# Expert weights loaded through two DMA queues instead of one, and the bias row selection copied by ScalarE instead of GpSimd

## The chip, the cores and the metric

The kernel runs on one core of a Trainium2 chip. The metric is the time of one execution on the device in microseconds (us): the median of a few runs. One execution was also profiled; its page and its trace are what this document reads. Engines are named as in the profile: PE is TensorE, PEld its weight loads, DVE is VectorE, ACT is ScalarE, POOL is GpSimd, SP is SyncE, which here does nothing but issue DMAs.

## The reference, cut to what matters

One encoder layer on 256 tokens of width 1024, in float32. A mixer part (three branches, gates, a projection, a layer norm) gives `h`. Then 32 experts of which each token takes 4:

```python
logits = hf @ w_router + b_router
top_val, top_idx = lax.top_k(logits, 4); top_w = softmax(top_val)
# for each expert e, on the tokens that chose it:
gu = xb @ w_gu[e] + b_gu[e]                       # (n, 1024) @ (1024, 2048)
gate, up = split(gu); gate = min(gate, 7); up = clip(up, -7, 7)
act = (up + 1) * (gate * sigmoid(1.702 * gate))
out = (act @ w_down[e] + b_down[e]) * weight      # (n, 1024) @ (1024, 1024)
# summed into the tokens, then h = LN(2**0.25 * h + sum)
```

The weights of all 32 experts (w_gu 8 MB and w_down 4 MB each) are read once, 384 MB in all.

## The kernel before, in words

The mixer comes first and lasts until about 320 us. The experts then go in 16 pairs, p = 0 to 15. Each expert has 64 places for tokens, so a pair fills the 128 rows of the PE's output: expert e of the pair has rows 64e to 64e+63, and `pair_mm` (line 1001) issues one matmul for each half.

For a pair, `up` (line 1007) makes the gate and up products in four PSUM tiles `gps` (128x512 each) over eight steps k. Before step 0 (for p = 0 after the last step) `add_bias` (line 992) adds the bias: a small tile `sel` picks row 2p and 2p+1 out of the bias rows by a matmul (lines 995 and 998). After the last step `swiglu` (line 808) runs twice: DVE takes the minimum (L809), ACT the sigmoid (L810), DVE the rest (L811 to L813). `down` (line 1056) begins with `add_bias` on two tiles `yps`, then runs eight steps on `w_down`; in its middle the tokens of the next pair are gathered (`gather`, L847 and L938). `transpose_act` (L1044, L1045), `weigh` (L946 to L955) and `combine` (L1078, L1082) follow.

The order is a pipeline: `up(p)`, then `down(p-1)` with `gather(p+1)` inside, then `transpose_act(p)`, `weigh(p)`, `combine(p-1)`, then `up(p+1)`. The whole loop stands inside `tc.manual_schedule` for DVE, PE and ACT: these three engines execute their instructions in the order in which the program writes them. Instructions of POOL and SP are placed by the scheduler, unless `keep_in_program_order` pins them.

The weights come in pieces of 2048 KB, twelve for a pair: eight of `w_gu` (`load_gu`, line 789) and four of `w_down` (`load_down`, line 800). They go round ten buffers ("ring0" to "ring9", `new_unit`, line 777), so a piece can be issued when the piece ten places before it has been used up. All are issued by SP, one after the other. From the third pair on, piece i of a pair holds two steps' rows of one expert: i even is the first expert of the pair, i odd the second, so that PE needs pieces 2j and 2j+1 together for steps 2j and 2j+1. For p < 2 and for the last two w_gu pieces of the last pair, one piece serves one step for both experts (`both`, line 784); the w_down pieces of pair 14 serve two steps for both experts each (`rows`). The last pair's w_down comes in twelve smaller pieces in `last_down` (line 1103), by SP. At p = 8, `norm_rows` (line 1129) selects the rows of the closing layer norm's parameters in the same way as `add_bias`.

Of the kernel before, what the change touches and what calls it, by code (L numbers as in the profile page):

```python
# [13 lines left out]
AF = mybir.ActivationFunctionType  # L14
# [762 lines left out]
def new_unit(K, shape):  # L777

    i = K.slot_no % K.NRING
    K.slot_no += 1  # L780
    return (K.early if i in K.EARLY else K.ring[i]).tile([128, *shape], F32, name="wexp", tag=f"ring{i}")


def both(p, k):

    return p < 2 or (p, k // 2) == (NE // 2 - 1, 3)


def load_gu(K, A, p, i, w=None):

    if (p, i) in K.loaded:
        return K.loaded[p, i]
    w = K.loaded[p, i] = w or new_unit(K, (2, 2 * D))
    src = A["w_gu"][0, 2 * p:2 * p + 2, i // 2 * 256:i // 2 * 256 + 256].rearrange("e (p k) n -> p e k n", p=128)
    src = src[:, :, i % 2] if both(p, i) else src[:, i % 2]
    K.tc.keep_in_program_order(K.nc.sync.dma_start(w, src))
    return w


def load_down(K, A, p, i, rows=False):  # L800

    w = new_unit(K, (2, 2, D) if rows else (4, D))
    src = A["w_down"][0, 2 * p:2 * p + 2, i // 2 * 512:i // 2 * 512 + 512].rearrange("e (p k) n -> p e k n", p=128)
    K.nc.sync.dma_start(w, src[:, :, i % 2 * 2:i % 2 * 2 + 2] if rows else src[:, i % 2])
    return w


# [9 lines left out]
def moe(ctx, K, A):  # L817
    tc, nc = K.tc, K.nc
# [122 lines left out]
    def weigh(p, P):  # L941

        bank = yps if p == 0 else mps if p == NE // 2 - 1 else gps
        t = bank()
        for tau in range(2):
            nc.tensor.transpose(t[:, tau * 128:tau * 128 + 128], P[:, tau].rearrange("p e s -> p (e s)"), K.ident)  # L946
        G = big.tile([128, S], F32R, name="G", tag="G", bufs=2)
        nc.scalar.activation(G, t[:, :S], AF.Copy)
        t = bank()
        for tau in range(2):  # L950
            nc.tensor.matmul(t[:, 0:2], P[:, tau].rearrange("p e s -> p (e s)"), wts[:, tau, 2 * p:2 * p + 2],
                             start=tau == 0, stop=tau == 1)
        w = big.tile([128, 1], F32, name="sw", tag="sw", bufs=2)
        for e in range(2):
            nc.scalar.activation(w[e * 64:e * 64 + 64], t[e * 64:e * 64 + 64, e:e + 1], AF.Copy)  # L955
        return G, w


    for p, k in [(p, k) for p in range(2) for k in range(8)][:K.NRING + 2]:
        if (p, k) not in ((0, 7), (1, 2)):  # L960
            load_gu(K, A, p, k)
    K.loaded[0, 7] = [big.tile([128, 2 * D], F32, name="wexp", tag=tag, bufs=1) for tag in ("work", "y")]
    for k, w in enumerate(K.loaded[0, 7]):
        nc.sync.dma_start(w, A["w_gu"][0, k, 768:1024].rearrange("(p k) n -> p k n", p=128)[:, 1])
    load_gu(K, A, 1, 2, K.res.tile([128, 2, 2 * D], F32, name="wexp", tag="sum", bufs=1))

    xT, P = gather(0, P0), P0
# [24 lines left out]
    def add_bias(acc, p, at, first):  # L992

        t = big.tile([128, 2, 64], F32, name="sel", tag="sel", bufs=2)
        nc.gpsimd.tensor_copy(t, K.rows[:, 2 * p:2 * p + 2, None].broadcast_to([128, 2, 64]))  # L995
        for ac, (r0, c0) in zip(acc, at):
            r = slice(r0, r0 + 32)
            nc.tensor.matmul(ac, t[r].rearrange("k e s -> k (e s)"), bias[r, c0:c0 + ac.shape[-1]], start=first,  # L998
                             stop=not first, skip_group_check=True)
# [7 lines left out]
    def up(p, xT, between=None, inside=None):  # L1007

        g = [(yps if p == 0 and n % 2 else gps)() for n in range(4)]
        early = p > 0  # L1010
        if early:
            add_bias(g, p, GU_ROWS, True)
        for k in range(8):
            if k % 2 == 0:
                ws = [load_gu(K, A, p, k + e) for e in range(2)]
            for n in (0, 2, 1, 3):
                cols = slice(n * 512, n * 512 + 512)
                if both(p, k):
                    w = ws[k % 2]
                    rows = [w[e][:, cols] if isinstance(w, list) else w[:, e, cols] for e in range(2)]  # L1020
                else:
                    rows = [w[:, k % 2, cols] for w in ws]
                pair_mm(g[n], xT, k, rows, not early and k == 0, early and k == 7)
            if inside and k == 6:
                inside()
        if not early:
            add_bias(g, p, GU_ROWS, False)
        if p == 0:
            K.work = big.tile([128, 2, D], F32, name="work", tag="work", bufs=1)
        if between:  # L1030
            between()
        a = K.work[:, 0]
        t = big.tile([128, 4, 512], F32, name="sg", tag="y", bufs=1)
        for i in range(2):
            swiglu(nc, t[:, i], t[:, 2 + i], a[:, i * 512:i * 512 + 512], g[i], g[2 + i])
        return a
# [19 lines left out]
    def down(p, aT, w, between=None):  # L1056
        yy = [yps() for _ in range(2)]
        add_bias(yy, p, DN_ROWS, True)
        for i in range(2):
            rows = p == NE // 2 - 2  # L1060
            ws = [load_down(K, A, p, i * 2 + e, rows) for e in range(2)]
            for k in range(4):
                for n in range(2):
                    c = slice(n * 512, n * 512 + 512)
                    w2 = [ws[k // 2][:, e, k % 2, c] if rows else ws[e][:, k, c] for e in range(2)]
                    pair_mm(yy[n], aT, i * 4 + k, w2, False, i * 4 + k == 7)
            if between and i == 0:
                between()
        y = new_y()
        for n in range(2):  # L1070
            leave(y, yy[n], w, slice(n * 512, n * 512 + 512))
        return y
# [56 lines left out]
    def norm_rows(gb):  # L1129

        t = big.tile([128, 2, 128], F32, name="nsel", tag="P", bufs=2)
        nc.gpsimd.tensor_copy(t, K.rows[:, 0:2, None].broadcast_to([128, 2, 128]))
        for r0, o in zip((64, 96), gb):
            for n in range(2):
                ps = mps()
                nc.tensor.matmul(ps, t[r0:r0 + 2, n], bias[r0:r0 + 2, 512:1024], start=True, stop=True)  # L1136
                nc.scalar.activation(o[:, n * 512:n * 512 + 512], ps, AF.Copy)
# [12 lines left out]
    with tc.manual_schedule(engines={mybir.EngineType.DVE, mybir.EngineType.PE, mybir.EngineType.Activation}):  # L1150
        P1 = choice(1)
        ahead = []
        a = up(0, xT, inside=lambda: ahead.append(gather(1, P1)))
        xT = ahead[0]
        for p in range(1, NE // 2):
            first = []
            a0, a = a, up(p, xT, (lambda: first.append(after(0, a, P))) if p == 1 else None)
            if p == 1:
                held = first[0]
                t = K.res.tile([128, 4, D], F32, name="sum", tag="sum", bufs=1)  # L1160
                z[:], gb = (t[:, 0], t[:, 1]), (t[:, 2], t[:, 3])
            P = P1
            if p < last:
                P1 = choice(p + 1)
                ahead = []
                y = down(p - 1, held[0], held[2], lambda: ahead.append(gather(p + 1, P1)))
                xT = ahead[0]
                now = after(p, a, P)
                if p == NE // 4:
                    norm_rows(gb)  # L1170
                back(y, p - 1, held[1])
                held = now
        G, w = weigh(last, P)
        now = []
        y = down(last - 1, held[0], held[2], lambda: now.extend((transpose_act(last, a, True), last_parts(last))))
        parts = now[1]
        st = last_down(last, now[0], G, w, parts, lambda: back(y, last - 1, held[1]))
        finish(K, A, [K.work[:, 0], K.work[:, 1]], st, *gb)
# [187 lines left out]
```

## Time and profile before

| what | us |
|---|---|
| median of 3 runs (1233.05 to 1233.71) | 1233.61 |
| the profiled execution's own time | 1233.55 |
| its span, first to last instruction | 1231.5 |
| PE busy | 1164.2 |
| DVE busy | 381.3 |
| ACT busy | 260.0 |
| POOL busy | 47.8 |
| q1 (SP's DMA queue), 456.62 MB, share of 16 DMA engines over the span | 90.5% |

The span is what the instructions cover; the execution's own time has about 2 us around it. Busy PE is not PE at its peak. A queue's share is the time that its packets took as a share of what 16 DMA engines have. "q1 hardware_dynamic" is the queue that SP fills, "q10" ACT's, "q0 software_dynamic" the one that POOL fills. A stage is read with the view by stretches: busy time of each engine, the clock granted to PE, the share of the DMA engines that was busy and the rate in GB/s.

### The profile page before, as it was taken

The numbers are of one execution on the slowest core, as the hardware profiler recorded it, in microseconds if no ns is written. First come the engines' busy times: TensorE is split into PE (matmuls) and PEld (weight loads), VectorE is DVE, ScalarE is ACT, GpSimd is POOL, SyncE is SP. The second block draws the span as 40 slices with busy tenths as digits, with TensorE's granted clock in tenths as the row PEclk, the third lists the DMA queues.
The fourth block names the chain that finished last, engine by engine and source line by source line (L and its number), as shares of the span: only waits on it lengthen the run. The fifth ranks groups of instructions, "written<-read, shape, count | busy, mean of one in ns | idle before, by whom it ended". The sixth has DMA issues, their size and how long they took to land.

```text
span 1231.5 us, 14887 instructions
## 1 busy us (share of the span) xinstructions
PE 1164.2 (95%) x6413; PEld 639.3 (52%) x6413; DVE 381.3 (31%) x591; ACT 260.0 (21%) x453; POOL 47.8 (4%) x70
## 2 busy tenths in 40 slices
PE   6999999999999999999989898999898989899995
PEld 6898999998544343443334242434243424333333
DVE  7995465486211131111202030211111111111124
ACT  4775555453111010100101010201010101000010
POOL 2150000000000000000000000000000000000000
PEclk8999999999999999999999999999999999999998
DMA  8755557687999999999999999999999999999994
GB/s 284 254 195 171 193 191 245 254 310 273 384 412 411 395 430 432 428 431 430 430 432 429 431 431 431 431 429 431 431 428 434 429 429 433 429 430 431 427 422 161
DMA packets 77241, 458.24 MB, mean 372 GB/s; under 512 B 4678, under 2 KB 39184, under 8 KB 50292
## 3 DMA queue, kind: packets, MB, share of 16 engines
q1 hardware_dynamic: 76712, 456.62, 90.5%
q8 instruction: 52, 0.85, 0.3%
q10 hardware_dynamic: 332, 0.56, 0.1%
q14 instruction: 17, 0.14, 0.0%
q0 software_dynamic: 128, 0.07, 0.0%
HBM read 456.18 MB, written 1.05 MB: 371 GB/s over the span
## 4 chain that ended last, share of the span: by engine, by line
PE 62%; DMA 34%; DVE 2%; ACT 1%; issue 0%; SPq 0%; POOL 0%; DVEq 0%; ACTq 0%
DMA wexp<-in_w_down_dram 27%; PE gps L1004 16%; PE yps L1004 15%; PE pj L146 7%; PE pj L145 7%; PE pj L144 7%; DMA wexp<-in_w_gu_dram 6%; PE mps L847 5%; PE gps L1044 1%; PE gps L998 1%; DVE wlo L118 1%; PE yps L1078 1%; PE mps L1078 1%; PE yps L998 1%; DMA first<-in_ln_in_b_dram 0%; PE mps L1136 0%
## 5 line engine op out<-in xcount | busy, mean ns | idle before, releaser
L1004 PE MATMUL gps<-wexp,xT 128*64 128x512 f32 x1984 | 447.9, 599 | 36.2 <-DMA wexp<-in_w_gu_dram 36.1
L1004 PEld LDWEIGHTS gps<-wexp,xT 128*64 128x64 f32 x1984 | 144.9, 138 | 335.1 <-issue 281.1
L1004 PE MATMUL yps<-wexp,work 128*64 128x512 f32 x960 | 220.7, 596 | 4.6 <-DMA wexp<-in_w_down_dram 4.6
L809 DVE TENSOR_SCALAR sg<-gps 128x512 f32<-128x512 f32 x31 | 21.3, 688 | 459.9 <-PE gps L1004 426.6
L1004 PEld LDWEIGHTS yps<-wexp,work 128*64 128x64 f32 x960 | 69.3, 137 | 142.9 <-issue 126.5
L118 DVE TENSOR_TENSOR wlo<-wraw,whi 128x1024 fp32r<-128x1024 f32 (+2 forms) x98 | 119.4, 1227 | 61.6 <-ACT whi L117 61.0
L810 ACT ACTIVATE sg<-sg 128x512 f32<-128x512 f32 x32 | 20.2, 630 | 489.1 <-DVE sg L809 489.1
L117 ACT ACTIVATE whi<-wraw 128x1024 fp32r<-128x1024 f32 (+2 forms) x98 | 95.4, 977 | 98.0 <-PE pj L145 82.1
L144 PE MATMUL pj<-hT,whi 128*128 128x256 f32 (+1 forms) x392 | 112.5, 287 | 0.0
L145 PE MATMUL pj<-hT,whi 128*128 128x256 f32 (+1 forms) x392 | 110.6, 282 | 0.3 <-DVE hT L118 0.3
L146 PE MATMUL pj<-hT,wlo 128*128 128x256 f32 (+1 forms) x392 | 110.6, 282 | 0.0
L1051 DVE SCALAR_TENSOR_TENSOR y<-yps,sw,y 128x512 fp32r<-128x512 f32 x30 | 22.5, 751 | 244.9 <-ACT y L1050 243.6
L145 PEld LDWEIGHTS pj<-hT,whi 128*128 128x128 f32 (+1 forms) x392 | 73.7, 188 | 1.0 <-DVE hT L118 0.8
L144 PEld LDWEIGHTS pj<-hT,whi 128*128 128x128 f32 (+1 forms) x392 | 73.7, 188 | 0.9 <-ACT whi L117 0.7
L146 PEld LDWEIGHTS pj<-hT,wlo 128*128 128x128 f32 (+1 forms) x392 | 73.6, 188 | 0.2
L847 PEld LDWEIGHTS mps<-P,h 128*128 128x128 f32 x512 | 61.6, 196 | 12.7 <-issue 12.2
L847 PE MATMUL mps<-P,h 128*128 128x128 f32 x512 | 64.8, 285 | 0.4 <-DVE P L840 0.4
L938 ACT ACTIVATE xT<-mps 128x512 f32<-128x512 f32 x32 | 19.1, 598 | 176.5 <-PE mps L847 176.5
L995 POOL COPY sel<-kp 128x128 f32<-128x128 f32 x32 | 9.5, 298 | 808.2 <-PE yps L998 483.3
L1050 ACT ACTIVATE y<-yps,sw 128x512 fp32r<-128x512 f32 x30 | 20.6, 688 | 88.1 <-PE yps L1004 78.7
L1082 DVE TENSOR_TENSOR sum<-sum,yps 128x512 f32<-128x512 f32 (+1 forms) x30 | 18.8, 666 | 22.1 <-PE yps L1078 22.1
L812 DVE TENSOR_TENSOR sg<-sg 128x512 f32<-128x512 f32 x32 | 22.1, 690 | 3.2 <-ACT sg L810 1.6
(279 smaller groups left out, 1049.3 us busy)
## 6 DMA issues: line engine op xcount, KB each, us to landing
wexp<-in_w_gu_dram SPq DMA_DIRECT2D x127, 2048.0 KB, 37.4
wexp<-in_w_down_dram SPq DMA_DIRECT2D x60, 2048.0 KB, 32.1
wraw<-in_w_in_dram SPq DMA_DIRECT2D x28, 1024.0 KB, 5.5
wexp<-in_w_down_dram SPq DMA_DIRECT2D x8, 768.0 KB, 16.4
wraw<-in_w_mem_kv_dram SPq DMA_DIRECT2D x4, 1024.0 KB
wraw<-in_w_br_gla_dram SPq DMA_DIRECT2D x4, 1024.0 KB
wraw<-in_w_out_dram SPq DMA_DIRECT2D x4, 1024.0 KB, 7.5
wraw<-in_w_br_fnet_dram SPq DMA_DIRECT2D x2, 1024.0 KB
```

Of the source, the lines that this page charges most:

```text
L117: K.nc.scalar.activation(hi, src, AF.Copy)
L118: K.nc.vector.tensor_tensor(lo, src, hi.bitcast(F32), ALU.subtract)
L144: nc.tensor.matmul(out, wh, xh, start=first, stop=False)
L145: nc.tensor.matmul(out, wh, xl, start=False, stop=False)
L146: nc.tensor.matmul(out, wl, xh, start=False, stop=last)
L809: nc.vector.tensor_scalar(g, gate, 7.0, None, ALU.min)
L812: nc.vector.tensor_tensor(g, g, s, ALU.mult)
L847: nc.tensor.matmul(t[:, c], h1[tau][:, f0 + c % 2:f0 + 256:2], P[:, tau].rearrange("p e s -> p (e s)"), start=first and c == 0, stop=last, ...
L998: nc.tensor.matmul(ac, t[r].rearrange("k e s -> k (e s)"), bias[r, c0:c0 + ac.shape[-1]], start=first, stop=not first, skip_group_check=True)
L1004: nc.tensor.matmul(acc[e * 64:e * 64 + 64], xT[:, k, e * 64:e * 64 + 64], w[e], start=first, stop=last, skip_group_check=True)
L1051: nc.vector.scalar_tensor_tensor(y[:, 1, sl], acc, w, y[:, 0, sl].bitcast(F32), ALU.mult, ALU.subtract)
L1078: nc.tensor.matmul(c, G[:, tau * 128:tau * 128 + 128], y[:, i, sl], start=i == 0, stop=i == 1)
```

## The change

In `load_gu`, odd pieces of pairs 2 to 15 are issued by POOL (`nc.gpsimd`) instead of SP. In `load_down`, odd pieces of pairs 1 to 14 are issued by POOL, and all pieces are pinned to program order. In `add_bias` and `norm_rows`, the copy that makes the selection tile is an ACT activation (Copy) instead of a POOL copy.

```diff
@@ load_gu
-    K.tc.keep_in_program_order(K.nc.sync.dma_start(w, src))
+    eng = K.nc.gpsimd if p > 1 and i % 2 else K.nc.sync
+    K.tc.keep_in_program_order(eng.dma_start(w, src))
@@ load_down
-    K.nc.sync.dma_start(w, src[:, :, i % 2 * 2:i % 2 * 2 + 2] if rows else src[:, i % 2])
+    eng = K.nc.gpsimd if p > 0 and i % 2 else K.nc.sync
+    K.tc.keep_in_program_order(eng.dma_start(w, src[:, :, i % 2 * 2:i % 2 * 2 + 2] if rows else src[:, i % 2]))
@@ add_bias
-        nc.gpsimd.tensor_copy(t, K.rows[:, 2 * p:2 * p + 2, None].broadcast_to([128, 2, 64]))
+        nc.scalar.activation(t, K.rows[:, 2 * p:2 * p + 2, None].broadcast_to([128, 2, 64]), AF.Copy)
@@ norm_rows
-        nc.gpsimd.tensor_copy(t, K.rows[:, 0:2, None].broadcast_to([128, 2, 128]))
+        nc.scalar.activation(t, K.rows[:, 0:2, None].broadcast_to([128, 2, 128]), AF.Copy)
```

## Rows read from the trace of the kernel before

**Rows 1.** The page: DMA queue (packets, MB, share) and the chain's shares by engine.
```profile
q1 hardware_dynamic: 76712, 456.62, 90.5%
...
PE 62%; DMA 34%; DVE 2%; ACT 1%; issue 0%; SPq 0%; POOL 0%; DVEq 0%; ACTq 0%
```

**Rows 2.** View by stretches: stretch, length, busy us of engines (instructions), PEclk, DMA share, GB/s.
```profile
320.00:420.00 100.00, 99.50 (x501) 40.77 (x502) 15.03 (x24) 11.25 (x22) 1.25 (x4) 1.00 0.96 396
360.00:380.00 20.00, 20.00 (x96) 6.75 (x94) 0.00 (x0) 0.00 (x0) 0.00 (x0) 1.00 0.99 392
410.00:420.00 10.00, 10.00 (x50) 3.40 (x48) 0.00 (x0) 0.00 (x0) 0.00 (x0) 1.00 0.93 365
420.00:560.00 140.00, 140.00 (x708) 57.38 (x704) 26.28 (x44) 15.08 (x30) 1.48 (x5) 1.00 1.01 429
560.00:1160.00 600.00, 560.70 (x2667) 225.56 (x2667) 99.44 (x165) 56.90 (x119) 6.62 (x22) 0.99 1.01 430
```

**Rows 3.** Waits of PE, 560 to 1160: total us, times, longest.
```profile
PE gps L1004 <- DMA wexp<-in_w_gu_dram: 34.8, 17, 2.7
```

**Rows 4.** Chain that ended last, 440 to 760: start us, us, what.
```profile
460.60 27.62 PE gps L1004 x128
...
512.01 27.62 PE gps L1004 x128
...
674.84 38.84 DMA wexp<-in_w_down_dram
...
733.20 38.84 DMA wexp<-in_w_down_dram
```

**Rows 5.** DMA issues of 380:396 and of 600:700: xcount, KB each, us to landing.
```profile
wexp<-in_w_gu_dram SPq DMA_DIRECT2D x3, 2048.0 KB, 9.8
...
wexp<-in_w_gu_dram SPq DMA_DIRECT2D x12, 2048.0 KB, 37.7
```

**Rows 6.** Timeline at up(0) to up(1): start us, us, instruction, [idle before, releaser].
```profile
355.30 27.69 PE L1004 MATMUL gps<-wexp,xT 128*64 128x512 f32 x128
...
356.35 0.63 ACT L810 ACTIVATE sg<-sg 128x512 f32<-128x512 f32 x1 [2.09 <-DVE sg L809]
```

**Rows 7.** Timeline at up(1) to down(0).
```profile
384.68 0.38 ACT L948 ACTIVATE G<-yps 128x256 fp32r<-128x256 f32 x1
...
385.21 1.25 PE L998 MATMUL yps<-ebias,sel 32*128 32x512 f32 x4 [0.50 <-ACT G L948]
...
388.06 0.63 ACT L810 ACTIVATE sg<-sg 128x512 f32<-128x512 f32 x1 [2.12 <-DVE sg L809]
```

**Rows 8.** Timeline at up(2) to down(1); the later pairs repeat it.
```profile
436.74 1.13 PE L998 MATMUL yps<-ebias,sel 32*128 32x512 f32 x4
...
437.79 0.63 ACT L810 ACTIVATE sg<-sg 128x512 f32<-128x512 f32 x1 [2.10 <-DVE sg L809]
```

**Rows 9.** Groups of ACT by form, 320 to the end: xcount | busy us, mean ns | idle.
```profile
L948 ACT ACTIVATE G<-gps 128x256 fp32r<-128x256 f32 x14 | 5.4, 386 | 0.0
L955 ACT ACTIVATE sw<-gps 64x1 f32<-64x1 f32 x28 | 4.6, 163 | 0.2
```

**Rows 10.** DMA queues in 17:23, where POOL's queue carries data: packets, MB, share.
```profile
q1 hardware_dynamic: 1178, 1.18, 62.7%
q0 software_dynamic: 128, 0.07, 3.9%
```

**Rows 11.** Timeline of POOL in the mixer: a DMA that POOL issues.
```profile
17.22 0.72 POOL L310 DMA_DIRECT2D gla<-in_w_decay_f_dram  x1 [1.83 <-DVE wlo L118]
```

**Rows 12.** Timeline of the end: down(14), then the last pair's last_down.
```profile
1183.54 3.65 PE L1004 MATMUL yps<-wexp,work 128*64 128x512 f32 x16 [0.29 <-DMA wexp<-in_w_down_dram]
...
1189.26 3.65 PE L1004 MATMUL yps<-wexp,work 128*64 128x512 f32 x16
1193.30 3.65 PE L1004 MATMUL yps<-wexp,work 128*64 128x512 f32 x16 [0.38 <-DMA wexp<-in_w_down_dram]
...
1200.85 2.79 PE L1004 MATMUL gps<-wexp,aT 128*64 128x512 f32 x14 [0.47 <-DMA wexp<-in_w_down_dram]
```

## The prediction, made before the changed kernel was run

> **What bounds the kernel now.** I read the page first: the chain that ended last is 62% PE and 34% DMA, and one DMA queue, SP's, moves nearly everything [rows 1]. So two resources take turns, and the next view must say where. The view by stretches does [rows 2]: from 420 to 1160 us the 16 DMA engines are busy at a share of 1.01 and move 429 to 430 GB/s, and PE has 560.7 us of work in the last 600. Before, from 320 to 420, PE is busy for 99.5 of 100 us and the DMA rate is only 396 GB/s. The chain agrees [rows 4]: up to 560 it runs through PE, one pair of experts in 512.01 - 460.60 = 51.4 us; later it returns to a `w_down` transfer once per pair, 733.20 - 674.84 = 58.4 us. Twelve pieces of 2.097 MB at 430 GB/s are 58.5 us, so the later pairs are paced by the DMA engines alone, a piece every 4.88 us, and PE has 58.4 - 51.4 = 7.0 us to spare in each; its waits for `w_gu` show most of them [rows 3].
>
> What the end of the kernel depends on is therefore the moment at which the DMA engines have moved the last byte, and the tail behind it. Three things can move that moment: the rate of the full stretch, what is lost in 320 to 420, and the tail. In 320 to 420 the loss is 100 x (430 - 396) / 430 = 7.9 us.
>
> **The change part by part.** The terms are added to the profiled execution's own time, 1233.55 us (span 1231.5 and about 2 around it), which is 0.06 below the median of the three runs; I call both 1233.6.
>
> *Two queues instead of one.* This adds and removes no bytes. What SP saves, half of its issues, is worth nothing: in 600 to 700 a piece lands 37.7 us after its issue, some eight pieces deep [rows 5], so issuing is never late there. Since PE needs pieces 2j and 2j+1 together and both buffers come free together, it does not matter whether they land one behind the other or side by side: the later one lands at the same time. For the rate I take no change: the DMA engines are at 1.01 with one queue [rows 2], and where both kinds of queue carried small packets, POOL's cost 3.9% of 16 x 6 us = 3.7 us for 0.07 MB, 53 us per MB, and SP's 62.7% = 60.2 us for 1.18 MB, 51 us per MB [rows 10]. Bounds: below, the 1% by which the share exceeds 1, that is 1% of 740 us, 7 us gained; above, 53/51 on half of the bytes, 2% of 740 us, 15 us lost. The value nearest to rows of the same packets is zero.
> The Trainium skill (DMA: Bandwidth & Descriptors, "Issuing engines are not separate DMA queues") says that DMAs of all issuing engines run on the same 16 DMA engines and that a second issuer saves only the issuing time. By that rule the first part of this change is worth nothing, and the trace agrees as far as one queue can show it: share 1.01.
>
> *POOL as issuer.* A DMA that POOL issued took POOL 0.72 us [rows 11]; six a pair are 4.3 us of 58, on an engine that does nothing else in the loop once the copies are gone. Behind a POOL DMA that waits for its buffer only later odd pieces stand. Taken as 0; if cover is gone, 0.7 us each at the places where the queue runs thin, at most 3 us.
>
> *The selection copy on ACT.* ACT keeps the order of the program. In `down(p-1)` the copy (L995) is written behind the two sigmoids of `swiglu(p)`; on POOL nothing stood in front of it. Its length lies between ACT's 0.16 us for 64x1 and 0.39 us for 128x256 [rows 9]; I take 0.28. Now PE must wait at the turn from `up` to `down`:
> - `up(0)` to `up(1)`: second sigmoid ends at 356.35 + 0.63 = 356.98, copy until 357.26, four bias matmuls of 1.13 us together [rows 8], so the first weight matmul starts at 358.4 instead of 355.30 [rows 6]: 3.1 us late.
> - `up(1)` to `down(0)`: 388.06 + 0.63 + 0.28 = 388.97 instead of 385.21 [rows 7]: 3.8 us, together 6.9.
> - every later turn: 437.79 + 0.63 + 0.28 = 438.70 instead of 436.74 [rows 8]: 2.0 us.
> At the start of `up(p)`, p > 1, the copy stands behind copies of `weigh` that PE has fed before `combine`; no wait. `norm_rows` happens once, in the full stretch: nothing.
>
> From 560 on, 2.0 us per pair lie inside PE's 7.0 spare microseconds: cost 0. Before 420 there is no such cover, because a late PE frees buffers late and the DMA queue is short: a piece issued in 380 to 396 lands after 9.8 us, two pieces' time [rows 5], so one piece is ahead of it and no more, and in 410 to 420 the share is 0.93, the engines ran out [rows 2]. There a late issue is a late transfer. Of the 6.9 us I count 6: the pieces issued before the second turn are only 3.1 late, and the piece ahead hides a little. After 420 the backlog grows by 7 us a pair, more than the 2 us that PE loses, and nothing more is lost. Bounds: 3 (only the first turn counts) to 9 (the third turn too). If PE's clock falls in those gaps, 1 to 2 us more; the rows show 1.00 after waits of 2.7 us [rows 2, 3].
>
> *The tail.* In `down(14)` a piece serves two steps alone, so that PE can begin when the first of two has landed. Now: the second lands at about 1183.5 and the fourth at 1193.3, for which PE waits 0.29 and 0.38 us [rows 12]. With the first and second sharing the engines, both land at the time of the second. The last half then starts at 1193.3 instead of 1189.26 and takes 2 x 3.65 = 7.3 us: 1200.6 instead of 1193.30 + 3.65 = 1196.95, 3.65 us late; the wait of 0.47 at 1200.85 [rows 12] swallows part. Taken as 3.2; bounds 0 (the queues don't share evenly and the first still lands first) and 5 (SP's last pieces take engine time from POOL's).
>
> Sum: 1233.6 + 6 + 3.2 = 1242.8, rounded to 1243.
>
> **The rivals.**
> *The second queue fills the gaps (faster).* Place: 320 to 420, where engines lack work. POOL's wait for its buffer no longer stands in SP's line, and two experts' rows are read at once. For it: 396 GB/s on average, and 392 at a share of 0.99 in 360 to 380 [rows 2], where packets were slow though the queue was not empty; another mix of addresses could cure that. Against: the buffers come free in PE's order, in twos, so there is seldom an odd piece that could go earlier. It decides if more than about 6 of the 7.9 us come back: all of it, and the copies without effect since the queue is then deeper, gives 1233.6 - 7.9 = 1225.7; with the tail 1229.
> *The queue of POOL is dearer.* Packets of two queues, or POOL's descriptors, slow the full stretch: up to 15 us on top of the forecast, 1258; half of that 1250. For it: 53 against 51. Against: that difference is within the rounding of 0.07 MB. The same page of the Trainium skill ("Measured (HBM→SBUF, 128 partitions, SWDGE, issued from GpSimd)") gives 425 GB/s for 16 MB from POOL; as an estimate, 430/425 on half of the bytes would be 0.6% of 740 us, 4 us more. No row here shows it.
> *The change does nothing that counts.* The late copies are hidden by more backlog than the one landing time shows, and the tail's pieces land in order: 1233.6, or up to 1236 with one of the two small.
>
> **How the numbers follow.** 0.2% of 1233.6 is 2.5 us, about what can be told from no change. Forecast (1238 to 1248 by its own bounds): 0.46. Dearer queue, 1248 to 1258: 0.15. Nothing that counts: 0.17. Gaps filled: 0.22. Slower is 0.46 + 0.15 = 0.61, the same 0.17, faster 0.22. The range reaches to the centre of the fast rival and most of the way into the dear one: 1227 to 1255, which leaves out some 0.05 below and 0.07 above.
>
> **What would show it.** Right: in the changed profile PE's first weight matmul of `up(1)` and `down(0)` comes 3 and 7 us later, with the selection copy on ACT as the releaser of L998 at each turn; the rate in 320 to 430 is lower than 396 or its end later; from then on 429 to 430 GB/s at a share of 1.0, split evenly between q1 and q0; a pair takes 58.4 us; PE reaches the end of `down(14)` later relative to the last transfer. Wrong: a rate in the full stretch away from 430 by over 1%; odd pieces landing long after even ones, with PE waiting for them; or bias matmuls that start as early as before.

## The result, and the profile after

The changed kernel takes 1248.08 us (median of 4 runs, 1245.91 to 1248.72) against 1233.66 before: a ratio of 1.0114, 95% interval 1.0099 to 1.0130, 14.4 us slower. The profiled execution took 1248.72 us, its span is 1246.9. The forecast was 1243, with a range of 1227 to 1255.

The page of the changed kernel, part 3: the queues, packets, MB, share of 16 DMA engines. One queue had 456.62 MB [rows 1]; now POOL's has 176.

```profile
q1 hardware_dynamic: 64232, 280.45, 56.1%
q0 software_dynamic: 12608, 176.24, 33.1%
```

The view by stretches of the changed kernel, to be laid beside [rows 2] (PE, PEld, DVE, ACT, POOL busy us; PEclk; DMA share; GB/s):

```profile
320.00:420.00 100.00, 91.47 (x444) 37.02 (x444) 13.96 (x23) 11.89 (x26) 2.81 (x5) 0.93 0.86 352
420.00:560.00 140.00, 134.84 (x652) 51.90 (x651) 24.09 (x40) 12.80 (x28) 8.67 (x16) 0.98 1.00 425
560.00:1160.00 600.00, 566.45 (x2705) 228.58 (x2706) 100.14 (x168) 65.81 (x147) 33.92 (x62) 0.98 1.01 431
```

From 560 on nothing has changed: 431 GB/s against 430. The loss stands in the first two rows. In 320 to 420 the rate fell from 396 to 352 GB/s, 100 x 44 / 430 = 10.2 us of full transfer; in 420 to 560 from 429 to 425, 140 x 4 / 430 = 1.3 us. That is 11.5 of the 14.4 us. PE's granted clock is 0.93 of full in the first stretch, where it was 1.00.

Waits of PE in the changed kernel, first 320 to 600, then 600 to 1180 (total us, times, longest). The releaser of the bias matmuls is now ACT's copy. Before, they waited once in 320 to 600, 0.50 us for another ACT instruction [rows 7]:

```profile
PE yps L1000 <- ACT sel L997: 9.8, 4, 4.2
PE gps L1000 <- ACT sel L997: 4.3, 1, 4.3
...
PE yps L1000 <- ACT sel L997: 18.8, 10, 2.1
PE gps L1006 <- DMA wexp<-in_w_gu_dram: 13.2, 15, 2.3
```

The waits for `w_gu` fell from 34.8 us [rows 3] to 13.2 (13.2 in 560 to 1160 too, the stretch of [rows 3]): what PE now waits for the copy, it waits less for the DMA.

The timeline of the changed kernel at the first turn, up(0) to up(1), against [rows 6] (lines from 796 on stand one or two further down than before: L997 is the copy, L1000 the bias matmul, L1006 the weight matmul):

```profile
355.96 0.63 ACT L812 ACTIVATE sg<-sg 128x512 f32<-128x512 f32 x1 [2.08 <-DVE sg L811]
356.50 0.29 ACT L997 ACTIVATE sel<-kp 128x128 f32<-128x128 f32 x1
...
356.84 2.09 PE L1000 MATMUL gps<-ebias,sel 32*128 32x512 f32 x8 [4.34 <-ACT sel L997]
...
358.86 6.32 PE L1006 MATMUL gps<-wexp,xT 128*64 128x512 f32 x20
```

And at the second, up(1) to down(0), against [rows 7]:

```profile
393.39 0.63 ACT L812 ACTIVATE sg<-sg 128x512 f32<-128x512 f32 x1 [2.09 <-DVE sg L811]
393.93 0.29 ACT L997 ACTIVATE sel<-kp 128x128 f32<-128x128 f32 x1
...
394.27 2.08 PE L1000 MATMUL yps<-ebias,sel 32*128 32x512 f32 x4 [4.19 <-ACT sel L997]
...
396.28 8.96 PE L1006 MATMUL yps<-wexp,work 128*64 128x512 f32 x32
```

The chain is the one foretold: second sigmoid, copy, bias matmuls. What was not in the sum is behind it: the bias matmuls take 2.08 us where [rows 8] have 1.13, and the first half of down(0) takes 8.96 us where the kernel before takes 7.09 for the same 32 matmuls:

```profile
386.38 7.09 PE L1004 MATMUL yps<-wexp,work 128*64 128x512 f32 x32
```

The view by stretches of 5 us of the changed kernel says why:

```profile
355.00:360.00 5.00, 3.16 (x12) 1.04 (x14) 2.91 (x5) 0.83 (x2) 0.00 (x0) 0.57 0.80 341
360.00:365.00 5.00, 5.00 (x18) 1.42 (x18) 0.00 (x0) 0.00 (x0) 0.00 (x0) 0.75 0.01 3
...
390.00:395.00 5.00, 0.81 (x3) 0.50 (x4) 3.50 (x6) 2.10 (x7) 0.00 (x0) 0.83 0.99 426
395.00:400.00 5.00, 5.00 (x14) 1.24 (x12) 0.88 (x3) 0.00 (x0) 0.00 (x0) 0.50 1.00 429
400.00:405.00 5.00, 5.00 (x24) 1.40 (x20) 0.00 (x0) 0.00 (x0) 0.00 (x0) 0.99 0.38 157
```

After each of the two waits PE's clock is at its lower level, 1.2 instead of 2.4 GHz (0.50 over the whole of 395 to 400; 0.57 and 0.75 are means over stretches with both levels). And the DMA engines run dry right behind: 3 GB/s in 360 to 365, 157 in 400 to 405. The kernel before, in the same stretches:

```profile
360.00:365.00 5.00, 5.00 (x26) 1.72 (x24) 0.00 (x0) 0.00 (x0) 0.00 (x0) 1.00 1.00 360
...
400.00:405.00 5.00, 5.00 (x27) 1.91 (x24) 0.59 (x1) 1.16 (x2) 0.00 (x0) 1.00 1.03 439
```

That the buffers come free late is seen in SP's waits for PE between 330 and 440, first before, then in the changed kernel (total us, times, longest). The longest grew from 14.3 to 20.0 us:

```profile
SPq L804 <- PE gps L1004: 25.2, 2, 14.3
...
SPq L806 <- PE gps L1006: 31.4, 2, 20.0
```

### The profile page after: what moved, and what is told of

Its sections match the earlier page's. It is cut to its first block, busy times and chain, and to the rows that moved or that the text cites. A ratio compares the mean times of both kernels' runs of the same rounds, so it can differ in the third digit from the quotient of the medians.

```text
span 1246.9 us, 14848 instructions
## 1 busy us (share of the span) xinstructions
PE 1172.2 (94%) x6413; PEld 637.5 (51%) x6413; DVE 380.9 (31%) x591; ACT 268.4 (22%) x486; POOL 83.4 (7%) x121
## 5 line engine op out<-in xcount | busy, mean ns | idle before, releaser
L1006 PE MATMUL gps<-wexp,xT 128*64 128x512 f32 x1984 | 445.5, 596 | 14.8 <-DMA wexp<-in_w_gu_dram 14.8
L1006 PEld LDWEIGHTS gps<-wexp,xT 128*64 128x64 f32 x1984 | 143.4, 137 | 313.3 <-issue 280.7
L1006 PE MATMUL yps<-wexp,work 128*64 128x512 f32 x960 | 228.2, 631 | 0.0
L1006 PEld LDWEIGHTS yps<-wexp,work 128*64 128x64 f32 x960 | 69.8, 145 | 147.4 <-issue 145.7
L118 DVE TENSOR_TENSOR wlo<-wraw,whi 128x1024 fp32r<-128x1024 f32 (+2 forms) x98 | 119.4, 1227 | 61.6 <-ACT whi L117 61.0
L849 PEld LDWEIGHTS mps<-P,h 128*128 128x128 f32 x512 | 61.6, 196 | 12.7 <-issue 12.2
L797 POOL DMA_DIRECT2D wexp<-in_w_gu_dram x56 | 30.6, 546 | 504.6 <-PE gps L1006 345.0
L1000 PE MATMUL yps<-ebias,sel 32*128 32x512 f32 x64 | 20.3, 712 | 30.5 <-ACT sel L997 30.5
L806 POOL DMA_DIRECT2D wexp<-in_w_down_dram x28 | 15.5, 554 | 310.9 <-PE gps L1006 164.7
```

What stands on the lines that cost most here:

```text
L118: K.nc.vector.tensor_tensor(lo, src, hi.bitcast(F32), ALU.subtract)
L797: K.tc.keep_in_program_order(eng.dma_start(w, src))
L849: nc.tensor.matmul(t[:, c], h1[tau][:, f0 + c % 2:f0 + 256:2], P[:, tau].rearrange("p e s -> p (e s)"), start=first and c == 0, stop=last, ...
L1006: nc.tensor.matmul(acc[e * 64:e * 64 + 64], xT[:, k, e * 64:e * 64 + 64], w[e], start=first, stop=last, skip_group_check=True)
```

## The experiments

Two theories. A, the late copy: the loss is PE's wait at the first turns and what follows it. B, the second queue: the loss is in sharing the engines, in POOL's issues or in the tail. All times are medians, each with its ratio to runs of the kernel before on the same chip and the 95% interval of that ratio. An interval reaches 1 to 2 us to either side, so a difference of two ratios is good to some 2 us. In the kernels with copies moved ahead, the copy stands in L998, the bias matmul in L1006 and the weight matmul in L1012.

**The copy alone, one queue.**

```diff
-    eng = K.nc.gpsimd if p > 1 and i % 2 else K.nc.sync
+    eng = K.nc.sync
-    eng = K.nc.gpsimd if p > 0 and i % 2 else K.nc.sync
+    eng = K.nc.sync
```

> The kernel before with one part of the change: the selection copies are on ScalarE in program order, all weight pieces stay on SyncE's queue. Theory A (the late copy: PE waits about 4 us at the first two turns for the copy that ACT executes behind the sigmoids, runs at half its clock for some us after each wait, frees buffers late while the DMA queue is thin): nearly all of the loss is here, 1244 to 1247 us, with 350 to 365 GB/s in 320 to 420 and waits of L1000 for the copy of 4.2 to 4.3 us at up(1) and down(0). Theory B (the second queue costs the time: pieces that share the engines, POOL's issues, the tail): 1234 to 1237 us.

Measured: 1248.14 us, ratio 1.0116 (1.0100 to 1.0131), the whole loss without any second queue. Its view by stretches repeats the changed kernel's:

```profile
320.00:420.00 100.00, 91.47 (x448) 36.96 (x444) 14.57 (x24) 11.89 (x26) 0.00 (x0) 0.93 0.87 355
420.00:560.00 140.00, 135.92 (x648) 52.04 (x644) 22.38 (x38) 12.35 (x27) 0.00 (x0) 0.96 1.00 425
```

Theory B falls as the main cause. The time is 1 us above A's range, which allowed the tail nothing.

**Two queues, the copies ahead of the sigmoids.** Same instructions on ACT, other places. `select(p)` is the tile and the copy that stood in `add_bias`; the diff is cut and has notes on the right:

```diff
+        t = early_sel.pop((p, at[0][1]), None) or select(p)     # in add_bias
...
         if early:                                               # in up
             add_bias(g, p, GU_ROWS, True)
+            if True:
+                early_sel[p - 1, 512] = select(p - 1)
...
+        if p == 0 and True:                                     # in up, ahead of swiglu
+            early_sel[1, 0] = select(1)
```

> The changed kernel with the two queues, but each selection copy on ACT is written ahead of the sigmoids it stood behind (the one for up(1) ahead of swiglu(0), the one for down(p-1) at the start of up(p)), so PE never waits for it. Theory A: the stretch 320 to 420 is back at 390 to 400 GB/s, and what is left is the tail's 2 to 4 us: 1235 to 1238 us. Theory B: 1244 to 1248 us, as the changed kernel.

Measured: 1236.28 us, ratio 1.0018 (1.0009 to 1.0028). The stretch is back:

```profile
320.00:420.00 100.00, 99.59 (x505) 41.30 (x505) 15.46 (x26) 12.96 (x28) 3.35 (x6) 1.00 0.97 397
420.00:560.00 140.00, 140.00 (x703) 56.81 (x700) 25.36 (x43) 15.17 (x32) 8.67 (x16) 1.00 1.01 430
```

So of 0.0114 the place of the 0.3 us copies in ACT's program is 0.0096, 11.8 us; 0.0018, 2.2 us, is left. One late copy remains in this and the other kernels, that for the bias of the last pair's `last_down`: PE waits 0.9 us for it.

**Which turns count.** Three kernels with two queues: the first two copies moved ahead (for up(1) and down(0)), the first alone, and only those of the later turns.

The diff is that of the kernel above, with other conditions:

```diff
+            if p == 1:                  # first two; first alone: if False; later turns: if p > 1
+                early_sel[p - 1, 512] = select(p - 1)
...
+        if p == 0 and True:             # later turns: if p == 0 and False
+            early_sel[1, 0] = select(1)
```

> The changed kernel with only the first two copies moved ahead (for up(1) and down(0)); the turns of pairs 2 to 15 keep the copy behind the sigmoids. Theory A says that the later turns are covered by the 7 us that PE has to spare per pair: within 2 us of the kernel with all copies moved, 1236 to 1240 us, though PE still waits 2 us at each of the 14 later turns. Rival: every turn costs, 14 x 2 us, minus what is covered: 1242 us or more. Theory B: 1244 to 1248 us.

> The changed kernel with the copy for up(1) alone moved ahead. The late copy costs 5.4 to 5.8 us of buffer release at each of the first two turns while the queue is thin, so half of the loss returns: 1241 to 1243 us. If the second turn's delay were covered by backlog, 1236 to 1238 us; if the first were, 1247 to 1248 us.

> The changed kernel with the copies of the turns of pairs 2 to 15 moved ahead, the first two left behind the sigmoids. If the later turns are covered, this stays at the changed kernel's time, 1245 to 1248 us; if their 14 waits of 2 us count, 1238 us or less.

Measured: first two 1235.87 us, ratio 1.0025 (1.0014 to 1.0036); first alone 1242.14 us, 1.0067 (1.0054 to 1.0080); later turns 1246.63 us, 1.0100 (1.0086 to 1.0115). As differences of ratios times 1234 us: the first turn costs 1.0114 - 1.0067, 5.8 us; the second 1.0067 - 1.0025, 5.2 us; the later ones 1.0025 - 1.0018, 0.9 us, or 1.0114 - 1.0100, 1.7 us, both inside the intervals. That the later turns are covered is seen in the kernel with the first two moved ahead, from 600 to 1180. PE waits ten times for the copy, and less for `w_gu` than the kernel before (34.8 us from 560 to 1160 [rows 3]). The fourteen later turns are these ten, three before 600 and one behind 1180:

```profile
PE yps L1006 <- ACT sel L998: 18.6, 10, 1.9
PE gps L1012 <- DMA wexp<-in_w_gu_dram: 12.6, 10, 1.7
```

So two waits of some 4 us cost 5.8 and 5.2 us while the queue is thin, and ten of 1.9 us cost nothing that these runs can tell once it is deep.

**PE busy while it waits.** The changed kernel with matmuls that nobody reads ahead of the first two late bias groups:

```diff
+        if p == 1:      # in up; in down: if p == 0
+            idle_t = mps()[:, :128]
+            for _ in range(18):
+                nc.tensor.matmul(idle_t, K.ident, K.ident, start=True, stop=True)
```

> The changed kernel with 18 extra matmuls of the identity (128x128, about 0.21 us each, into a tile that nothing reads) on PE ahead of the bias matmuls of up(1) and of down(0): PE waits as long as before but is busy while it waits. If the granted clock that fell to 0.50 to 0.75 after these two waits is part of the loss (2.5 to 3 us of work at half rate after each), it stays at 1.00 and 1242 to 1244 us come out; if the waits alone are the loss, 1247 to 1249 us.

Measured: 1242.79 us, ratio 1.0080 (1.0066 to 1.0094); its interval does not touch the changed kernel's 1.0099 to 1.0130. The same stretches of this kernel:

```profile
355.00:360.00 5.00, 4.88 (x29) 1.81 (x29) 1.67 (x3) 0.55 (x2) 0.00 (x0) 1.00 0.54 229
360.00:365.00 5.00, 5.00 (x26) 1.70 (x24) 0.00 (x0) 0.00 (x0) 0.00 (x0) 1.00 0.75 252
...
395.00:400.00 5.00, 5.00 (x30) 2.51 (x27) 0.00 (x0) 0.00 (x0) 0.54 (x1) 1.00 0.87 301
```

The clock stays at 1.00, and 1.0114 - 1.0080, 4.2 us, come back: the clock's share of the first two turns. The DMA engines still run dry in part (229 and 252 GB/s), since the wait for the copy is still there: the rest, 11.0 - 4.2 = 6.8 us.

How late PE is behind both turns can be read directly. From the first bias matmul of up(0) to the gather in the middle of down(0), in the kernel before, the changed one and this one:

```profile
351.75 0.69 PE L998 MATMUL gps<-ebias,sel 32*128 32x512 f32 x1
393.40 4.04 PE L847 MATMUL mps<-P,h 128*128 128x128 f32 x32
...
351.37 0.69 PE L1000 MATMUL gps<-ebias,sel 32*128 32x512 f32 x1
405.17 4.04 PE L849 MATMUL mps<-P,h 128*128 128x128 f32 x32
...
350.13 0.69 PE L1000 MATMUL gps<-ebias,sel 32*128 32x512 f32 x1
398.35 4.04 PE L849 MATMUL mps<-P,h 128*128 128x128 f32 x32
```

That is 41.65, 53.80 and 48.22 us. The changed kernel is 12.2 us late, and 11.0 were lost; with its clock kept up it is 6.6 us late, and 6.8 were lost.

**The pieces that share the engines at the end.** Two queues, copies ahead, but the last two w_gu pieces of pair 15 and the w_down pieces of pair 14 all by SP:

```diff
-    eng = K.nc.gpsimd if p > 1 and i % 2 else K.nc.sync
+    eng = K.nc.gpsimd if p > 1 and i % 2 and not both(p, i) else K.nc.sync
-    eng = K.nc.gpsimd if p > 0 and i % 2 else K.nc.sync
+    eng = K.nc.gpsimd if p > 0 and i % 2 and not rows else K.nc.sync
```

> Two queues, all copies moved ahead, and the pieces that serve steps alone (the last two w_gu pieces of pair 15 and the w_down pieces of pair 14) all on SyncE's queue again. If the 2.3 us that the kernel with all copies moved ahead is slower than before come from pieces that share the engines at the end, 1233 to 1235 us, and PE begins the second half of down(14) when its first piece has landed; if they come from the second queue in the loop or from the copies on ACT, 1236 to 1237 us as without this edit.

Measured: 1233.66 us, ratio 0.9992 (0.9983 to 1.0000), against 1.0018 with shared pieces. PE in the two kernels, first with the pieces shared (the last two steps of up(15), then down(14)):

```profile
1175.25 8.78 PE L1012 MATMUL gps<-wexp,xT 128*64 128x512 f32 x32 [2.40 <-DMA wexp<-in_w_gu_dram]
...
1185.73 7.09 PE L1012 MATMUL yps<-wexp,work 128*64 128x512 f32 x32
```

and with SP's alone, where up(15) runs through and down(14) starts on its first piece:

```profile
1163.52 14.86 PE L1012 MATMUL gps<-wexp,xT 128*64 128x512 f32 x64 [0.32 <-DMA wexp<-in_w_gu_dram]
...
1180.08 3.65 PE L1012 MATMUL yps<-wexp,work 128*64 128x512 f32 x16
1184.63 3.65 PE L1012 MATMUL yps<-wexp,work 128*64 128x512 f32 x16 [0.90 <-DMA wexp<-in_w_down_dram]
```

Where the pieces are shared, PE waits for both at 1175 and starts down(14) at 1185.73 instead of 1180.08. Of these 5.65 us, 1.0 was there when up(15) began (1149.21 against 1148.17). The clock has a part: the 32 matmuls behind the wait of 2.40 us took 8.78 us, where 7.09 is usual, at a mean granted clock of 0.66 in 1175 to 1180. 1.0018 + 0.0008 = 0.0026, 3.2 us, is the price of the shared pieces. No run separates the `w_gu` pieces from the `w_down` pieces.

**One queue, copies on ACT and ahead.** The two edits together that the first two experiments made singly.

> One queue (SyncE's), selection copies on ACT, all moved ahead: the second half of the change alone without its wait. If the remaining 2.3 us belong to the second queue, this equals the kernel before, 1233 to 1235 us; if they belong to copies on ACT, 1236 to 1237 us.

Measured: 1233.44 us, ratio 0.9996 (0.9987 to 1.0005). Copies on ACT cost nothing where nothing stands ahead of them, and beside 0.9992 the second queue neither costs nor gains anything in the loop. The pinning of `load_down`, the third part of the change, is in this kernel too.

**One queue, only the last copy late.** As the one-queue kernel just above, with `if p < NE // 2 - 1:` ahead of the line that selects for down(p-1).

> One queue, copies on ACT and moved ahead, except at the last turn (down(14) after up(15)), where it stands behind the sigmoids and two copies of weigh. The kernel with the late copies and one queue loses as much as the one with two, though it has no pieces that share the engines at the end. If the late copy costs the tail what the sharing costs it (2 to 3 us), 1235.5 to 1237 us; if a wait of 2 us there is covered, as the forecast had it, 1233 to 1234.5 us.

Measured: 1235.39 us, ratio 1.0010 (0.9999 to 1.0021), against 0.9996: 1.7 us, but the intervals overlap. It is a hint, not a result: the tail of one queue may pay 1 to 2 us for its last late copy, which would explain why the copy alone with one queue lost as much as the change with two. That the two prices do not add where the pieces are shared, because PE waits for those anyway, is not shown.

No kernel was clearly faster than the one before; the two at 0.9992 and 0.9996 equal it.

## Why the prediction was right, and which term was mis-sized

The number alone would not tell: 1248.1 lies where the forecast's own bounds (1238 to 1248) meet those of the dearer queue (1248 to 1258). What decides is the kernel with the copy alone, which loses as much without a second queue.

*The bound and the two queues: right.* The full stretch stayed at 430 to 431 GB/s. From 600 to 700 the two queues of the changed kernel split it evenly (packets, MB, share):

```profile
q0 software_dynamic: 1472, 21.50, 50.3%
q1 hardware_dynamic: 1468, 21.43, 50.0%
```

By the Trainium skill's rule (DMA: Bandwidth & Descriptors, "Issuing engines are not separate DMA queues") there was no bandwidth to win. The trace agrees: 430 GB/s from two queues as from one. The rival of a dearer POOL queue is refuted by the same rows. The Trainium skill (DMA: Bandwidth & Descriptors, "Measured (HBM→SBUF, 128 partitions, SWDGE, issued from GpSimd)") gives 425 GB/s for 16 MB issued from GpSimd. No run here has POOL's queue alone; with half of the bytes on it the rate is 430. The rival of filled gaps fails too: with no late copy, two queues move 397 GB/s in 320 to 420 and one 396 [rows 2].

*POOL as issuer: right.* It was put at 0; an issue took POOL about 0.55 us in the loop (56 issues of `w_gu`, 30.6 us busy), and two queues without late copies and shared pieces equal one.

*The late copy: right in place, too small in size.* The delays were forecast at 3.1, 3.8 and 2.0 us, with the instruction that causes them; the copy took 0.29 us, the estimate was 0.28. The term of the sum that was mis-sized is the 6 us by which these waits delay the last transfer: it measured 11.0 (5.8 for the first turn, 5.2 for the second), above its bounds of 3 to 9. 6.8 of them are what was summed: with the clock kept up PE was 6.6 us late behind both turns, where 6.9 were forecast. The other 4.2 are the clock, which the forecast set aside as "1 to 2 us more" with the argument that the rows show 1.00 after waits of 2.7 us. The rows do not show that: the stretch with those waits has a mean of 0.99 [rows 2]. Of its eight waits of 2.6 to 2.7 us three have slow matmuls behind them (the last section shows one), and none of its waits is as long as 4 us.

*The later turns: right.* Covered, 0.9 to 1.7 us inside the intervals; the waits for the DMA shrank by about what the copy took. The forecast took 7.0 us of cover per pair and read most of it in PE's waits. The rows show less: PE is idle for 39.3 of 600 us [rows 2], 3.8 in each pair of 58.4. It was enough.

*The tail: right in cause and size, not in place.* 3.2 us were forecast, 3.2 measured for the shared pieces. But the forecast had PE wait for the `w_down` pieces of `down(14)`. What shows is a wait of 2.40 us for the last two `w_gu` pieces, in up(15), and the slower clock behind it; in down(14) PE then waits for no piece. That the sizes agree to the tenth is luck.

The sum with the measured terms is 1233.7 + 11.0 + 3.2 = 1247.9; measured were 1248.1. This is no check: the terms are differences of ratios of these same kernels. For the copy alone with one queue the sum is a check: 1233.7 + 11.0 and the 1.7 us that are only hinted at, 1246.4, inside that kernel's interval but 1.7 us below its median. The profiled executions hold a candidate for this remainder. Behind the last turn the bias matmuls and the first half of down(14) took 2.08 and 9.41 us with the copy alone, and 1.33 and 8.54 where only the last copy was late: 1.6 us more at the lower clock. It is one execution of each, so it is not shown.

## What to carry to other kernels

On an engine that keeps the program's order, an instruction costs its place, not its length: before an instruction is moved to another engine, look at what the queue there waits for when the consumer needs it, and write it ahead of that wait. The same PE delay is free where a transfer queue is deep and paid nearly in full where it is thin (12.2 us late, 11.0 lost): read the share and the landing times of the stretch in which the instruction lies, not the mean. And price a new PE wait with the time that PE may run at its lower clock afterwards.

## What the runs showed of the hardware that was not expected

PE's clock fell after some waits of 1.9 to 2.7 us and not after others of the same length. In the kernel with the copy alone, at the last turn, PE waited 1.90 us for the copy; the stretches behind it:

```profile
1190.00:1195.00 5.00, 3.73 (x8) 1.03 (x10) 1.58 (x3) 1.16 (x5) 0.00 (x0) 0.62 1.00 423
1195.00:1200.00 5.00, 5.00 (x20) 1.56 (x18) 0.00 (x0) 0.00 (x0) 0.00 (x0) 0.70 1.00 422
```

There too the 32 matmuls behind it took 9.41 us instead of 7.09. Yet of the ten waits of 1.85 to 2.12 us in the changed kernel from 600 to 1180, four have 7.09 us behind them and six 8.2 to 8.8. In the kernel before, two waits of 2.67 us for weights, with weight matmuls on both sides:

```profile
704.05 7.08 PE L1004 MATMUL gps<-wexp,xT 128*64 128x512 f32 x30 [2.67 <-DMA wexp<-in_w_gu_dram]
...
938.85 8.53 PE L1004 MATMUL gps<-wexp,xT 128*64 128x512 f32 x30 [2.67 <-DMA wexp<-in_w_gu_dram]
```

So neither the length of the wait nor the kind of matmuls around it decides alone. No run separates what does; it stays open. The Trainium skill (TensorE: Matmul & The Clock Gate, "Part 1") says that the clock has two levels only and that an idle PE falls to the lower. The 0.50 over 395 to 400 agrees.

The DMA engines lose about as much as PE is late: behind the two waits they moved 3 and 157 GB/s over 5 us, and SP's longest wait for a buffer grew by 5.7 us, from 14.3 to 20.0, because the buffer that the next piece needs is freed by the matmuls that came late and slow. What was lost is near PE's delay of 12.2 us, not more.
